# First MLP of a two-layer diffusion backbone: row sums moved from GpSimd to VectorE, background pieces placed by hand, two small rows loaded later

## Chip, cores and metric

The kernel runs on one core of a Trainium2 chip. The metric is the device time of one execution in microseconds (us); lower is better. The five engines of the core are called as in the profile: PE is TensorE, DVE is VectorE, ACT is ScalarE, POOL is GpSimd, SP is SyncE, which here only issues transfers. Each engine executes its own instructions strictly in their order; an instruction that waits holds up everything behind it on the same engine or issuing queue.

## What is computed

Two layers act on 512 latent tokens and 256 context tokens of width 1024. Layer 0 mixes tokens by pooling, layer 1 by attention; each is followed by an MLP with squared ReLU. The reference, cut to the part that the change touches (layer 0's MLP, on all 768 tokens):

```python
def ada_mods(cond, w, b):
    m = (jax.nn.silu(cond) @ w + b)[..., None, :]
    return jnp.split(m, N_MOD, axis=-1)
...
def sq_relu_mlp(h, w_in, w_out):
    return jnp.square(jax.nn.relu(h @ w_in)) @ w_out      # w_in 1024 x 4096, w_out 4096 x 1024
...
    m_lat = sq_relu_mlp(modulate(rms_norm(x, g_mlp_pre[i]), sh2, sc2), w_mlp_in[i], w_mlp_out[i])
    x = x + gt2 * rms_norm(m_lat, g_mlp_post[i])
```

The same MLP is applied to the context rows. `ada_mods` gives the shifts, scales and gates of each sub-layer; it needs silu(cond) for two conditioning vectors, `c` and `c_ctx`.

## The kernel before

**Precision.** Every float32 product is made of three products of halves: each operand is split into a rounded part (a CAST on ACT) and a remainder (a subtraction on DVE), and hi*hi + hi*lo + lo*hi is summed in PSUM.

**Front (0 to about 105 us).** Row norms, the pooling mixer and the conditioning of layer 0 run in an order written out by hand. SP streams the conditioning weights `w_ada` in 1 MB loads through a ring of six buffers (`raw_load`). `silu_rows` (L990) belongs to this kernel's later part but its four transfers carry no place of their own: for each of the two conditioning vectors, one writes silu(cond) as 1024 single floats to DRAM (`silu<-cond`, L992), and one reads that row back into all 128 partitions (`crow<-silu`, L993). The compiler's scheduler put the two writes at 12.54 us of the SP queue.

**First phase of the first MLP (about 105 to 387 us), `mlp0` (L1007).** The 4096 hidden columns are done in 16 rounds g of 256. Rounds 0 and 1 are plain. Rounds 2 to 15 use a seven-product scheme (Strassen's, in Winograd's form): instead of eight block products of half size, a round makes seven, each of 12 matmuls of 128x384 (`Seven`, L811; one such group is called a *half product* here, numbered 0 to 6). Half products 0, 2, 4 and 6 add into one PSUM bank `a`; between them ACT has to copy that bank out: `sc.copy(b, a)` after 0, `sc.copy(c, a)` after 2 (half product 4 may only start when that copy has read the bank), `sc.copy(r1[:, HN:TOK], a)` after 4 (half product 6 waits for it). At the end ACT applies ReLU and squares the two hidden rows into `hiddens[g % 2]`.

Between the half products, `behind(0)` to `behind(6)` issue background pieces:

- `weights_sums(g + 1, raw)` (L762) returns six steps that prepare the weights of the next round: `put` B11 (cast on ACT, remainder on DVE), `difference` (two DVE subtractions t1, t2 into a work tile), `put` T1 T2, `difference2` (t3, t4, into a second work tile; t4 reads the first one for the last time), `put3` T3 T4, `put3` B22.
- `asked` holds two calls of `ada_dot` (L340) per round: dot products of rows of `w_ada` with the rows `crow`, on DVE, two instructions (one per conditioning vector) for each call in rounds 2 to 13, one in rounds 14 and 15.

All pieces stand in one list, spread evenly: with eight pieces, `behind(0)` gets the first two, and the two dot calls come last, in `behind(5)` and `behind(6)`.

Work tiles rotate through three buffers (`work_tile`, L184). In one round they are first used in the order: t1/t2, `r1`, t3/t4, `r0`; so the ReLU into `r0` needs the buffer of t1/t2.

**Row sums.** Each pair of rounds (even, odd) gives the four quarters of a left operand of the second phase. `left_sums` (L975) runs after every odd round and before round 2 (seven times): POOL computes four sums of 128x768, and issues seven transfers per pair to DRAM (`lefts`), the three quarters and the four sums. Everything in this stretch is pinned to the written order on every engine (`pin(True)`).

**Loads.** A round asks SP for the weights of round g + 2 and then for the `w_ada` block of round g + 1. Both use a ring of three 1 MB buffers (`rawp`). Ahead of round 2 one of the three is held by the hidden rows of round 0 (`early`) until the first row sums have read them.

**Second phase, `Halves` (L1057, about 387 to 595 us).** The product with w_out again takes seven products per pair of rounds, in four passes, `PASSES = ((0, 4), (2, 5), (6, 3), (1,))`. A pass goes over the seven pairs with one or two of the products; each product keeps three PSUM banks for the whole pass, taken from two pools of four. `load` runs five products ahead, `prepare` three. At the last pair `take` (L1125) moves banks to SBUF; in product 5 it needs `self.banks[2]`, the banks of product 2.

Of the kernel before, what the change touches and what calls it, by code (L numbers as in the profile page):

```python
# [17 lines left out]
P = 128  # L18
# [79 lines left out]
def backbone(ctx: ExitStack, tc, x, ctx_in, w_ada, w_pool, w_qkv, g_q, g_k, w_o, w_mlp_in,  # L98
# [85 lines left out]
    def work_tile():  # L184
        return tmp.tile([P, D], F32, tag="t", name="work")
# [625 lines left out]
    class Seven:  # L811
# [10 lines left out]
        def run(self, behind):  # L822
            pool, tag = ((psB, "b"), (psA, "s"))[self.pool]
            b, a, c, e = (pool.tile([P, 512], F32, tag=tag, name="psin")[:, 0:HN] for _ in range(4))
            r0, r1 = (work_tile()[:, 0:TOK] for _ in range(2))
# [6 lines left out]
            self.chain(e, 1, True, True)  # L832
            sc.copy(r1[:, 0:HN], e)
# [4 lines left out]
            self.chain(b, 3, False, True)  # L838
            sc.activation(r0[:, 0:HN], b, AF.Relu)
# [49 lines left out]
    def keep(store, key, fn, *args):  # L889
        store[key] = fn(*args)  # L890
# [83 lines left out]

    def left_sums(p, even, odd):  # L975
        a11, a21, a12, a22 = (z[:, :, HN * h:HN * h + HN] for z in (even, odd) for h in range(2))
        s1, s2, s3, s4 = combined
        keep = lambda n, z: gp.dma_start(two(lefts[:, p, n]), z)
        def one(n, d, a, b, op):
            gp.tensor_tensor(out=d, in0=a, in1=b, op=op)  # L980
            keep(n, d)
        keep(0, a11)
        keep(1, a12)
        keep(3, a22)
        one(4, s1, a21, a22, ALU.add)
        one(5, s2, s1, a11, ALU.subtract)
        one(6, s3, a11, a21, ALU.subtract)
        one(2, s4, a12, s2, ALU.subtract)

    def silu_rows():  # L990
        for c in range(2):
            sy.dma_start(silu[c].rearrange("(k p) -> p k", p=P), cond[:, :, c])  # L992
            sy.dma_start(crow[:, c], silu[c].partition_broadcast(P))  # L993
# [7 lines left out]
    PASSES = ((0, 4), (2, 5), (6, 3), (1,))  # L1001
# [5 lines left out]
    def mlp0(inner, order, last, before_last):  # L1007
# [10 lines left out]
        inner = Inner(1, wi, hH, hL, hiddens[1], chunks0, TOK)  # L1018
        pinned[0] = False
        silu_rows()  # L1020
# [7 lines left out]
        left_sums(0, early, hiddens[1])  # L1028
        chain = Halves()
        for g in range(2, NG):  # L1030
            seven = Seven(products, hiddens[g % 2], g % 2, g < 4)
            pieces = []
            if g < NG - 1:
                steps, products = weights_sums(g + 1, raw)
                pieces += steps
            if asked:
                pieces += asked.pop(0)
            if g < NG - 2:
                raw = raw_load(w_mlp_in[0, g + 2])
            if g < NG - 1:  # L1040
                ask(*work.pop(0))
            else:
                chain.begin()
                pieces += [lambda: None] * 2 + [lambda: chain.prepare(0), lambda: None, lambda: chain.prepare(1)]
            n = len(pieces)
            seven.run(lambda z: [f() for f in pieces[(n * z + 6) // 7:(n * z + n + 6) // 7]])
            if g % 2 and g < 2 * PAIRS:
                left_sums(g // 2, *hiddens)
            if g == 4:
                head_gains()  # L1050
        chain.run()
# [5 lines left out]
    class Halves:  # L1057
# [67 lines left out]
        def take(self, n, q, ps):  # L1125
            c11, c12, c21, c22 = (accv[:, 2 * q + h, 512 * c:512 * c + 512] for h in range(2) for c in range(2))
            add = lambda d, a, b, op=ALU.add: ve.tensor_tensor(out=d, in0=a, in1=b, op=op)
            if n in (0, 4):
                sc.copy(c11 if n == 0 else c12, ps)
            elif n == 5:  # L1130
                add(c21, c11, ps)
                add(c22, c21, c12)
                add(c12, c22, self.banks[2][q])
            elif n == 6:
                add(c21, c21, ps)
                add(c22, c22, ps)
            elif n == 3:
                add(c21, c21, ps, ALU.subtract)
            elif n == 1:
                add(c11, c11, ps)  # L1140
# [202 lines left out]
    def head_gains():  # L1343
        tc.keep_in_program_order(sy.dma_start(grow[:, 0, :], g_q[0].partition_broadcast(P)))
        tc.keep_in_program_order(sy.dma_start(grow[:, 1, :], g_k[0].partition_broadcast(P)))
        ve.tensor_scalar(out=grow[:, 0, :], in0=grow[:, 0, :], scalar1=float(HD) ** -0.5, scalar2=None, op0=ALU.mult)
# [509 lines left out]
```

## Time and profile before

| quantity | value |
|---|---|
| median of 3 runs | 1198.72 us (1197.62 to 1199.57) |
| the profiled execution's own time | 1200.45 us |
| its span, first to last instruction | 1198.7 us, mean granted TensorE clock 0.974 |
| PE busy | 1124.0 us, 94% |
| DVE busy | 950.6 us, 79% |
| ACT busy | 618.0 us, 52% |
| POOL busy | 157.6 us, 13% |

How to read what the prediction quotes. A timeline row is: start in us from the span's start, duration in us, engine, line, operation, output<-input, partitions x elements, count, and in brackets the idle time just before it with what ended it. L94 is the line of a helper that records instructions in order, so rows are told apart by tile: `raw` is a loaded weight block, `work` a work tile, `units` and `rb` homes of prepared weights, `psin` the PSUM banks of the first phase, `pso` those of the second, `waste` the dots. A row of the waits view gives total wait, number of times and the longest. A row of the windows view gives a stretch, its length, then busy time (count) of PE, PEld (weight loads), DVE, ACT and POOL, the granted clock (1.00 is full), the share of the DMA engines and GB/s. A row of a DMA list ends with KB per transfer and the median time from issue to landing. A row of the groups gives total busy us and the mean ns of one.

### The profile page before, as it was taken

The page shows a single profiled execution, that of the slowest core. Times are in us where ns is not written, and L with a number is a line of the kernel's source. Part 1 is how long each engine was busy: PE and PEld are TensorE (multiplying, and loading weights), DVE is VectorE, ACT ScalarE, POOL GpSimd, SP SyncE. Part 2 cuts the span into 40 slices and gives each one's busy share as a digit, 9 for nine tenths or more (in the row PEclk, how much of TensorE's full clock was granted, in tenths as well). Part 3 has the DMA queues.
Part 4 walks back from the last instruction along what each step waited for, and adds up shares of the span by engine and source line. Part 5 has one row for each costly group of instructions (what it writes and reads, how often), then busy time and mean ns, then how long its engine had stood idle before and what let it go on. Part 6 is the DMA issues. An engine that isn't in the chain of part 4 may idle for free.

```text
span 1198.7 us, 15810 instructions
## 1 busy us (share of the span) xinstructions
PE 1124.0 (94%) x6030; PEld 979.7 (82%) x6030; DVE 950.6 (79%) x1291; ACT 618.0 (52%) x1035; POOL 157.6 (13%) x204
## 2 busy tenths in 40 slices
PE   7799789887898999899999999999999999999997
PEld 6479679877798787678888889998998888888886
DVE  5488888888886888898669678978687788779786
ACT  6387444434454553445358447764577345445523
POOL 1050332133321000000022220001200000000001
PEclk9899899888998999999999999999999999999999
DMA  9893555454557799997722210105334132313203
GB/s 365 281 388 118 185 198 188 156 210 180 202 176 270 303 366 393 383 361 271 279 110 71 71 36 19 61 28 193 123 125 157 36 141 108 110 64 141 106 19 122
DMA packets 52507, 213.13 MB, mean 178 GB/s; under 512 B 7408, under 2 KB 10304, under 8 KB 37840
## 3 DMA queue, kind: packets, MB, share of 16 engines
q1 hardware_dynamic: 45824, 185.52, 42.4%
q0 software_dynamic: 6608, 26.61, 5.7%
q8 instruction: 47, 0.77, 0.3%
q14 instruction: 28, 0.23, 0.1%
HBM read 178.16 MB, written 33.96 MB: 177 GB/s over the span
## 4 chain that ended last, share of the span: by engine, by line
PE 70%; DVE 15%; ACT 6%; issue 4%; DMA 3%; POOL 2%; SPq 0%; DVEq 0%; POOLq 0%; ACTq 0%
PE psin L682 14%; PE pso L94 12%; PE pso L1261 11%; PE psin L94 8%; DVE work L94 5%; PE pso L949 4%; PE psq L1385 4%; PE psy L1669 3%; PE po L1645 3%; DMA raw<-in_w_ada 3%; PE pss L1604 3%; DVE waste L94 3%; DVE units L94 3%; ACT units L94 2%; PE pspt L1626 2%
## 5 line engine op out<-in xcount | busy, mean ns | idle before, releaser
L94 PE MATMUL pso<-ra,sums 128*128 128x512 f32 x594 | 137.2, 390 | 3.8 <-DVE acc L94 3.5
L94 PEld LDWEIGHTS pso<-ra,sums 128*128 128x128 f32 x594 | 111.1, 188 | 28.8 <-DVE acc L94 4.3
L94 DVE CUSTOM_DVE_ANT_0 waste<-raw,crow 128x1024 f32<-128x1024 f32 (+1 forms) x72 | 88.1, 1224 | 8.5 <-DMA raw<-in_w_ada 6.8
L682 PE MATMUL psin<-ra,rb 128*128 128x512 f32 (+1 forms) x310 | 87.8, 360 | 0.0
L242 POOL TENSOR_SCALAR ms<-ss 128x1 f32<-128x1 f32 x15 | 9.7, 648 | 566.1 <-ACT junk L229 546.1
L1261 PE MATMUL pso<-units,pairs 128*128 128x512 f32 x336 | 82.7, 389 | 0.0
L682 PE MATMUL psin<-ra 128*128 128x512 f32 (+1 forms) x256 | 76.5, 376 | 0.0
L94 ACT CAST ra<-work 128x1024 fp32r<-128x1024 f32 x34 | 35.6, 1047 | 75.6 <-DVE work L94 73.9
L1261 PEld LDWEIGHTS pso<-units,pairs 128*128 128x128 f32 x336 | 63.1, 188 | 13.1
L1265 DVE TENSOR_TENSOR acc<-acc,pso 128x512 f32<-128x512 f32 x72 | 48.7, 682 | 26.2 <-PE pso L1261 26.2
L94 PE MATMUL psin<-sums,rb 128*128 128x384 f32 x70 | 27.8, 539 | 42.0 <-ACT psin L94 42.0
L94 PE MATMUL psin<-ra,units 128*128 128x384 f32 x340 | 63.5, 334 | 0.0
L682 PEld LDWEIGHTS psin<-ra,rb 128*128 128x128 f32 x310 | 55.6, 189 | 8.7
L94 PE MATMUL psin<-sums,units 128*128 128x384 f32 x336 | 61.2, 335 | 1.3 <-DVE units L772 0.6
L94 PEld LDWEIGHTS psin<-sums,units 128*128 128x128 f32 x336 | 58.3, 188 | 2.2 <-DVE units L772 1.0
L94 PE MATMUL pso<-ra,rb 128*128 128x512 f32 x252 | 58.6, 390 | 0.9 <-DVE ra L94 0.9
L94 PEld LDWEIGHTS psin<-ra,units 128*128 128x128 f32 x340 | 59.3, 188 | 0.0
L94 PEld LDWEIGHTS psin<-sums,rb 128*128 128x128 f32 x70 | 22.3, 327 | 44.2 <-ACT psin L94 44.2
L94 DVE TENSOR_TENSOR ra<-work,ra 128x1024 fp32r<-128x1024 f32 x34 | 41.7, 1225 | 19.3 <-ACT ra L94 19.3
L682 PE MATMUL psin<-rb,rb 128*128 128x512 f32 (+1 forms) x155 | 55.9, 362 | 0.6 <-DVE rb L1738 0.6
L94 PEld LDWEIGHTS pso<-ra,rb 128*128 128x128 f32 x252 | 47.2, 188 | 11.1 <-DVE ra L94 1.3
L94 ACT CAST units<-work 128x1024 fp32r<-128x1024 f32 x17 | 17.7, 1047 | 73.8 <-DVE work L94 67.8
(329 smaller groups left out, 2835.4 us busy)
## 6 DMA issues: line engine op xcount, KB each, us to landing
raw<-in_w_ada SPq DMA_DIRECT2D x48, 1024.0 KB, 10.3
raw<-in_w_mlp_in SPq DMA_DIRECT2D x32, 1024.0 KB, 5.1
lefts<-acc POOLq DMA_DIRECT2D x48, 384.0 KB, 3.3
raw<-in_w_mlp_out SPq DMA_DIRECT2D x18, 1024.0 KB, 5.5
wide<-lefts SPq DMA_DIRECT2D x38, 384.0 KB, 7.0
wide<-in_w_mlp_out SPq DMA_DIRECT2D x21, 512.0 KB, 7.0
halfway<-work POOLq DMA_DIRECT2D x14, 512.0 KB, 6.6
raw<-in_w_mlp_out SPq DMA_DIRECT2D x14, 512.0 KB, 7.3
```

Source lines behind the costliest of these rows:

```text
L94: return lambda *args, **kw: self.tc.keep_in_program_order(f(*args, **kw))
L242: gp.tensor_scalar(out=ms[:, 0:1], in0=ss[:, parts - 1:parts], scalar1=rest, scalar2=EPS, op0=ALU.add, op1=ALU.add)
L682: te.matmul(ps[:, bank, o:o + ln], w[:, k, fs], rhs, start=start, stop=(k == KT - 1 and n == 2), skip_group_check=len(ks) < KT or self.paired)
L949: te.matmul(pss[h][:, 0:cols[h][1]], a[:, f, ts_], w[:, f, cols[h][0]:sum(cols[h])], start=(n == 0 and not seeded[t]), stop=(n == len(seq) ...
L1261: te.matmul(ps, a, w, start=(m == 0), stop=(m == len(seq) - 1))
L1265: ve.tensor_tensor(out=M[n][:, t], in0=M[n][:, t], in1=ps, op=ALU.add)
L1385: te.matmul(ps, a[:, k, sl], w[:, k % 4, :], start=(k == 0 and n == 0), stop=(k == KT - 1 and n == 2))
L1604: te.matmul(ps[:, c2, 0:384], a[:, sl], b[:, kv, 384 * c2:384 * c2 + 384], start=(n == 0), stop=(n == 2))
L1626: te.transpose(ps[:, j, :], p[:, k * P:(k + 1) * P], ident)
L1645: te.matmul(po[:, 0:256], v, p, start=(n == 0), stop=(n == len(seq) - 1))
L1669: te.matmul(ps, a[:, k, sl], w[:, k % 4, o:o + width], start=(k == 0 and n == 0), stop=(k == KT - 1 and n == 2))
```

## The change

- `left_sums` no longer runs as a block on POOL. The four sums become four pieces for DVE, placed in the next even round behind half products 3, 4, 5 and 5. The transfers to `lefts` stay on POOL; the first quarter's is issued one round earlier (`left_keep`).
- The background pieces get fixed places: the six weight steps behind half products 0, 0, 1, 2, 3, 4; the two dot calls behind 1 and 6 (before: 5 and 6 in rounds with eight pieces). In the list behind half product 1 the dots stand after `put` T1 T2, ahead of `difference2`.
- `silu_rows` is called before the pin of the loads ends, and its four transfers are kept in the program's order on SP: behind the load of round 2's weights.
- `r1` and `r0` are taken from the rotation where they are first written.
- In the second phase the second pass handles product 5 before product 2; the addition into `c12` moves from product 5 to product 2.
- A scaling of `grow` moves from round 4 to round 8.

```diff
--- before.py
+++ after.py
@@ -822,7 +822,6 @@
         def run(self, behind):
             pool, tag = ((psB, "b"), (psA, "s"))[self.pool]
             b, a, c, e = (pool.tile([P, 512], F32, tag=tag, name="psin")[:, 0:HN] for _ in range(4))
-            r0, r1 = (work_tile()[:, 0:TOK] for _ in range(2))
             (wH, _), (aH, _) = self.products[0]
             for z in (b, c) if self.fresh else ():
                 te.matmul(z, wH[0], aH[0], start=True, stop=True, skip_group_check=True)
@@ -830,12 +829,14 @@
             sc.copy(b, a)
             behind(0)
             self.chain(e, 1, True, True)
+            r1 = work_tile()[:, 0:TOK]
             sc.copy(r1[:, 0:HN], e)
             behind(1)
             self.chain(a, 2, False, False)
             sc.copy(c, a)
             behind(2)
             self.chain(b, 3, False, True)
+            r0 = work_tile()[:, 0:TOK]
             sc.activation(r0[:, 0:HN], b, AF.Relu)
             behind(3)
             self.chain(a, 4, False, False)
@@ -972,25 +973,26 @@
     hiddens = [two(acc[:, 2 * TOK * q:2 * TOK * q + 2 * TOK]) for q in range(2)]
     combined = [two(acc[:, 4 * TOK + TOK * n:5 * TOK + TOK * n]) for n in range(4)]
 
+    def left_keep(p, n, z):
+        gp.dma_start(two(lefts[:, p, n]), z)
+
     def left_sums(p, even, odd):
         a11, a21, a12, a22 = (z[:, :, HN * h:HN * h + HN] for z in (even, odd) for h in range(2))
         s1, s2, s3, s4 = combined
-        keep = lambda n, z: gp.dma_start(two(lefts[:, p, n]), z)
+
         def one(n, d, a, b, op):
-            gp.tensor_tensor(out=d, in0=a, in1=b, op=op)
-            keep(n, d)
-        keep(0, a11)
-        keep(1, a12)
-        keep(3, a22)
-        one(4, s1, a21, a22, ALU.add)
-        one(5, s2, s1, a11, ALU.subtract)
-        one(6, s3, a11, a21, ALU.subtract)
-        one(2, s4, a12, s2, ALU.subtract)
+            ve.tensor_tensor(out=d, in0=a, in1=b, op=op)
+            left_keep(p, n, d)
+
+        left_keep(p, 1, a12)
+        left_keep(p, 3, a22)
+        return [lambda: one(4, s1, a21, a22, ALU.add), lambda: one(5, s2, s1, a11, ALU.subtract),
+                lambda: one(6, s3, a11, a21, ALU.subtract), lambda: one(2, s4, a12, s2, ALU.subtract)]
 
     def silu_rows():
         for c in range(2):
-            sy.dma_start(silu[c].rearrange("(k p) -> p k", p=P), cond[:, :, c])
-            sy.dma_start(crow[:, c], silu[c].partition_broadcast(P))
+            tc.keep_in_program_order(sy.dma_start(silu[c].rearrange("(k p) -> p k", p=P), cond[:, :, c]))
+            tc.keep_in_program_order(sy.dma_start(crow[:, c], silu[c].partition_broadcast(P)))
 
     asked = []
 
@@ -998,7 +1000,7 @@
         raw = raw_load(w_ada[i, m, j])
         asked.append([lambda b=b: ada_dot(i, m, j, nc_, raw, [crow[:, c] for c in range(nc_)], waste, b) for b in range(2)])
 
-    PASSES = ((0, 4), (2, 5), (6, 3), (1,))
+    PASSES = ((0, 4), (5, 2), (6, 3), (1,))
 
     def pin(on):
         for z in (ordered, mixed, queued):
@@ -1016,8 +1018,8 @@
         raw = raw_load(w_mlp_in[0, 2])
         steps, products = weights_sums(2, raw)
         inner = Inner(1, wi, hH, hL, hiddens[1], chunks0, TOK)
+        silu_rows()
         pinned[0] = False
-        silu_rows()
         for z in steps:
             z()
         inner.run()
@@ -1025,29 +1027,40 @@
         ask(*work.pop(0))
         sum_banks(True)
         pin(True)
-        left_sums(0, early, hiddens[1])
+        left_keep(0, 0, early[:, :, 0:HN])
+        due = left_sums(0, early, hiddens[1])
         chain = Halves()
         for g in range(2, NG):
             seven = Seven(products, hiddens[g % 2], g % 2, g < 4)
-            pieces = []
+            behind = [[] for _ in range(7)]
             if g < NG - 1:
                 steps, products = weights_sums(g + 1, raw)
-                pieces += steps
+                for n, z in enumerate(steps):
+                    behind[(0, 0, 1, 2, 3, 4)[n]].append(z)
+            if g % 2 == 0:
+                for n, z in enumerate(due):
+                    behind[(3, 4, 5, 5)[n]].append(z)
             if asked:
-                pieces += asked.pop(0)
+                for n, z in enumerate(asked.pop(0)):
+                    behind[(1, 6)[n]].append(z)
             if g < NG - 2:
                 raw = raw_load(w_mlp_in[0, g + 2])
             if g < NG - 1:
                 ask(*work.pop(0))
             else:
                 chain.begin()
-                pieces += [lambda: None] * 2 + [lambda: chain.prepare(0), lambda: None, lambda: chain.prepare(1)]
-            n = len(pieces)
-            seven.run(lambda z: [f() for f in pieces[(n * z + 6) // 7:(n * z + n + 6) // 7]])
-            if g % 2 and g < 2 * PAIRS:
-                left_sums(g // 2, *hiddens)
+                behind[4].append(lambda: chain.prepare(0))
+                behind[6].append(lambda: chain.prepare(1))
+            seven.run(lambda z: [f() for f in behind[z]])
+            if g < 2 * PAIRS:
+                if g % 2:
+                    due = left_sums(g // 2, *hiddens)
+                else:
+                    left_keep(g // 2, 0, hiddens[0][:, :, 0:HN])
             if g == 4:
                 head_gains()
+            if g == 8:
+                ve.tensor_scalar(out=grow[:, 0, :], in0=grow[:, 0, :], scalar1=float(HD) ** -0.5, scalar2=None, op0=ALU.mult)
         chain.run()
         pin(False)
         sum_banks(False)
@@ -1130,7 +1143,8 @@
             elif n == 5:
                 add(c21, c11, ps)
                 add(c22, c21, c12)
-                add(c12, c22, self.banks[2][q])
+            elif n == 2:
+                add(c12, c22, ps)
             elif n == 6:
                 add(c21, c21, ps)
                 add(c22, c22, ps)
@@ -1343,7 +1357,6 @@
     def head_gains():
         tc.keep_in_program_order(sy.dma_start(grow[:, 0, :], g_q[0].partition_broadcast(P)))
         tc.keep_in_program_order(sy.dma_start(grow[:, 1, :], g_k[0].partition_broadcast(P)))
-        ve.tensor_scalar(out=grow[:, 0, :], in0=grow[:, 0, :], scalar1=float(HD) ** -0.5, scalar2=None, op0=ALU.mult)
 
     kTH = kTL = vH = vL = early = None
```

## Prediction

> **What bounds the kernel now.** I read the page first (PE busy 94% of the span), then the waits of PE, then the windows of the first MLP, then the timeline of each engine over one even and one odd round.
>
> ```profile
> PE psin L94 <- ACT psin L94: 42.4, 8, 6.4
> 146.77:372.47 225.70, 190.17 (x1012) 187.37 (x1011) 189.93 (x227) 99.34 (x156) 70.96 (x66) 0.91 0.52 185
> ```
>
> PE's one large wait is that of the half products for a copy on ACT. Rounds 3 to 14, six pairs, take 225.7 us, 37.6 a pair, at a granted clock of 0.91. One even round on four engines, from its fourth half product:
>
> ```profile
> 280.76 2.25 PE L94 MATMUL psin<-ra,units 128*128 128x384 f32 x12
> 289.08 0.69 PE L94 MATMUL psin<-sums,rb 128*128 128x384 f32 x1 [6.08 <-ACT psin L94]
> 293.09 2.45 PE L94 MATMUL psin<-rb,rb 128*128 128x384 f32 x12
> 287.61 1.04 ACT L94 CAST units<-work 128x1024 fp32r<-128x1024 f32 x1 [8.20 <-DVE work L94]
> 282.45 2.29 DVE L94 TENSOR_TENSOR work<-raw 128x512 f32<-128x512 f32 x1
> 284.78 2.79 DVE L94 TENSOR_TENSOR work<-raw,work 128x512 f32<-128x512 f32 x1
> 282.16 2.04 POOL L94 TENSOR_TENSOR acc<-acc 128x768 f32<-128x768 f32 x1
> 285.20 1.81 POOL L94 TENSOR_TENSOR acc<-acc 128x768 f32<-128x768 f32 x1
> ```
>
> The chain reads backwards. PE waits 6.08 us for the copy into `c`; on ACT that copy stands behind a cast, which waited 8.20 us for DVE's t2; t1 and t2 took 2.29 and 2.79 us, ending just after POOL's sums end (284.20, 287.01). So POOL's row sums hold DVE up, and DVE holds PE. The odd round, which has no POOL sums:
>
> ```profile
> 301.73 1.23 DVE L94 TENSOR_TENSOR units<-raw,units 128x1024 fp32r<-128x1024 f32 x1 [0.43 <-ACT units L94]
> 303.59 0.69 DVE L94 TENSOR_TENSOR work<-raw,work 128x512 f32<-128x512 f32 x1
> 305.40 1.23 DVE L94 TENSOR_TENSOR units<-work,units 128x1024 fp32r<-128x1024 f32 x1 [1.12 <-ACT units L94]
> 307.15 0.69 DVE L94 TENSOR_TENSOR work<-raw,work 128x512 f32<-128x512 f32 x1
> 307.95 0.49 ACT L94 ACTIVATE work<-psin 128x384 f32<-128x384 f32 x1 [2.20 <-DVE work L94]
> 309.28 0.48 ACT L94 COPY work<-psin 128x384 f32<-128x384 f32 x1
> 309.41 1.23 DVE L94 TENSOR_TENSOR rb<-work,rb 128x1024 fp32r<-128x1024 f32 x1 [1.58 <-ACT rb L94]
> 308.01 2.24 PE L94 MATMUL psin<-rb,ra 128*128 128x384 f32 x12
> 310.09 2.24 PE L94 MATMUL psin<-ra 128*128 128x384 f32 x12
> 312.09 1.22 DVE L94 CUSTOM_DVE_ANT_0 waste<-raw,crow 128x1024 f32<-128x1024 f32 x1
> 314.96 0.48 ACT L94 COPY psin<-psin 128x384 f32<-128x384 f32 x1
> 315.37 1.05 ACT L94 CAST units<-raw 128x1024 fp32r<-128x1024 f32 x1
> 317.04 2.86 DVE L94 TENSOR_TENSOR units<-raw,units 128x1024 fp32r<-128x1024 f32 x1
> ```
>
> Without POOL beside it t2 takes 0.69 us. A half product takes 310.09 - 308.01 = 2.08 us; after the stop in the even round it was 293.09 - 289.08 = 4.01: the clock is lower there for a while. DVE goes from the first remainder (301.73) to that of the next round (317.04) in 15.3 us and ends without a gap before it; seven half products of 2.08 us are 14.6. DVE, not PE, already sets the pace of a round, with two waits for ACT in it (1.12 and 1.58). That decides what the change can give.
>
> **First MLP, even rounds.** Off: four POOL sums. On: four DVE sums of 768 elements.
>
> ```profile
> L94 DVE TENSOR_TENSOR sums<-wide,sums 128x768 fp32r<-128x768 f32 x28 | 26.7, 952 | 0.0
> 137.94 0.69 PE L94 MATMUL psin<-sums,rb 128*128 128x384 f32 x1 [6.45 <-ACT psin L94]
> 135.90 0.33 SPq L94 DMA_DIRECT2D raw<-in_w_mlp_in  x1
> DMA to landing us min/median/max: 4.7/5.0/6.8
> ```
>
> The nearest row gives 0.95 us each, four are 3.8 (at 1.23, the price of a 1024-wide one, 4.9). All else stays on DVE: 15.3 + 3.8 = 19.1 us for an even round. The sums stand behind half products 3 to 5, so the weight steps ahead of the critical copy run at their short times, and the 6.08 us stop goes. The seven transfers per pair stay on POOL; nothing waits behind them there, and the first quarter's is merely earlier.
>
> **First MLP, all rounds: the dots moved up.** Two dots (half of 312.09 to 317.04, 2.5 us) now lie on DVE ahead of t3 and t4. Who waits: the ReLU into `r0` takes the buffer of t1/t2, which t4 reads last (the 2.20 row). Behind that ReLU on ACT stand the cast of T3 T4 and the copy `r1` that half product 6 needs. From the first remainder to the ReLU is 307.95 - 301.73 = 6.2 us, now 8.7. From the ReLU to the end of that copy, 309.76, is 1.8; half product 6 starts then; from its start (310.09) through the last ReLUs, squares and the copy to the next round's first cast, ending 316.42, is 6.3; hand-overs 0.1. Sum 8.7 + 1.8 + 6.3 + 0.1 = 16.9 us. This loop exceeds DVE's own 15.3 and sets the odd rounds; in the even ones 19.1 is longer. The price of the move is thus 0 to 1.6 us per pair; I take 1.6, as every link has a row.
>
> A pair becomes 19.1 + 16.9 = 36.0 us against 37.6: 6 x 1.6 = 10 us saved. Round 2 loses its 6.45 us stop and 1.9 of slow products and gets a stop of 2.2 before half product 6 (2.5 of dots less the 0.3 in hand between 309.76 and 310.09): 6 saved. Against it: `early` is now read by the third sum, behind half product 5, and not by POOL at 136; the load that took its buffer at 135.90 goes out some 8 us later, lands 5 us after, and round 3's first cast waits about 3 (0 to 5). Sum for this phase: -10 - 6 + 3 = -13, between -28 (dots and load cost nothing, and the sums overlap a little) and -4 (the DVE sums cost 4.9 a pair, the load 5).
>
> The stops of PE that remain are thus some 2.2 us. [...]
>
> **Front: the silu rows.**
>
> ```profile
> 12.54 15.38 SPq L992 DMA_DIRECT2D silu<-cond  x2
> 28.02 12.77 SPq L179 DMA_DIRECT2D raw<-in_w_ada  x6
> DMA packets 2203, 0.88 MB, mean 68 GB/s; under 512 B 2097, under 2 KB 2097, under 8 KB 2097
> silu<-cond SPq DMA_DIRECT2D x2, 4.0 KB, 25.0
> 37.16 1.94 PE L94 MATMUL psada<-raw,cond 128*32 128x256 f32 x16 [5.58 <-DMA raw<-in_w_ada]
> 43.55 1.21 PE L94 MATMUL psada<-raw,cond 128*32 128x256 f32 x16 [2.65 <-DMA raw<-in_w_ada]
> 89.56 13.47 SPq L179 DMA_DIRECT2D raw<-in_w_mlp_in  x2
> 126.93 1.04 ACT L94 CAST units<-raw 128x1024 fp32r<-128x1024 f32 x1
> q1 hardware_dynamic: 1805, 8.87, 48.7%
> ```
>
> The two silu writes block the SP queue from 12.54 to 28.02, and in the DMA list of 28 to 41 us (the packet row) the core moves only 68 GB/s, with 2097 tiny packets. PE waits 5.58 + 2.65 = 8.2 us and then runs slow (sixteen products 1.94 us at first, 1.21 later: 0.7), which I count twice, 1.5, as the clock is still returning at 43.55. With the writes gone the loads follow one another. I take -10; bounds -12 (nearly all of the 13 us) and -5. In their new place the rows stand between the two loads of the 89.56 row, which then go at about 80 and 93; round 2's first cast of the second block (126.93) is then at 117. The two writes, at 13 us for both, and the wait of each read for its write fit into these 37 us, and the DMA list of 74 to 124 us (the last row) has its hardware queue busy only 48.7%: 0.
>
> **Second phase.**
>
> ```profile
> 509.98 1.66 PE L94 MATMUL pso<-ra,sums 128*128 128x512 f32 x6 [3.07 <-DVE acc L94]
> 512.03 5.75 PE L94 MATMUL pso<-ra,sums 128*128 128x512 f32 x24 [0.39 <-DVE acc L94]
> 448.61 0.69 SPq L94 DMA_DIRECT2D raw<-in_w_ada  x1
> 457.47 1.23 DVE L94 CUSTOM_DVE_ANT_0 waste<-raw,crow 128x1024 bf16<-128x1024 f32 x1 [1.16 <-DMA raw<-in_w_ada]
> ```
>
> After the second pass PE waits 3.07 + 0.39 = 3.5 us for the additions that free product 2's and 5's banks. With 5 first, its additions lie beside product 2, and product 2's beside product 6 of the next pass: -3.5. In exchange the buffer that a pair's load reuses is read last by product 2's remainder; from 5's subtraction to there lie two remainders of about 0.95 and one or two of 1.2, some 3 us. SP issues the `w_ada` load behind it, and the dots already wait 1.16 us for that (issued 448.61). Two buffers alternate, so at most 1.5 us per pair come through; I take half, over six pairs 4.5, and 0 if the three products prepared ahead hide it. Together +1, between -3.5 and +5.5. `grow`, moved to round 8, is one small instruction, free in both places.
>
> **Sum.** Against the profiled execution's 1200.45 us: -10 - 13 + 1 = -22, 1178.5. That execution lies 1.73 above the median shown, 1198.72; the forecast for the median is 1176.7. Own range: low 1200.45 - 12 - 28 - 3.5 - 1.7 = 1155; high 1200.45 - 5 - 4 + 5.5 - 1.7 = 1195.
>
> **Rivals.**
> - *Products set the pace.* If DVE's waits for ACT were filled, a pair would be fourteen half products, 29.1 us: 6 x 8.5 + 8 for round 2, less 3 for the load, is -56; with -10 and -3.5 the time is 1129. Against it: the odd rounds run without POOL and are at DVE's 15.3, not PE's 14.6. Chance 0.07.
> - *The first MLP gives nothing*: rounds about 1.1 us longer than worked out, as hand-overs on DVE and ACT add up. 1200.45 - 10 + 1 - 1.7 = 1190. For it: the forecast saves only 1.6 of 37.6 us a pair. Chance 0.12.
> - *The front's gain is lost*: the rows written in singles hold SP up again, now ahead of rounds 2 and 3's loads. The writes took 25 us to land at their old place; two of those behind each other and 5 for the load are 55 us where 37 are at hand, 18 too long: up to 1195. Against it: the half idle queue there. Chance 0.11.
> - *Slower: the clock falls at the short stops.* If 2.2 us idle are enough, half product 6 and the next 0 take 2.08 more each. In odd rounds both lie on the loop: after half product 6 (over at 312.33) ACT has only 2.6 us of its own, to 314.96, against the slower 4.2 of half product 0, so +2.1 and +1.6; in even rounds DVE's longer list leaves about +1.6. Per pair 5.3, with round 2 33 us in all: 1200.45 - 10 - 13 + 1 + 33 - 1.7 = 1210. It decides if stops of 2.2 us suffice. Against it: the stop of 3.07 us at 509.98 was followed by 24 products of 0.24 us, hardly slower than usual. Chance 0.07.
>
> The forecast's own chance is 0.60, and 0.03 is left for no change.
>
> **How the numbers follow.** The likeliest case gives 1176.7. The range 1155 to 1195 takes in its bounds and the two rivals on the near side; left out are the products' pace, the clock and the rest, 0.17. The measurement tells about 0.2% (2.4 us, so 1196.3) from no change. Faster: 0.60 + 0.07 + 0.12 + 0.09 of the third rival = 0.88; same: 0.03 + 0.02 = 0.05; slower 0.07.
>
> **What would show it.** Right: no POOL arithmetic between 125 and 375 us; t1 and t2 at 0.69 us in every round; PE's waits for ACT in the first MLP in many pieces near 2 us, before half product 6, in place of seven near 6; a pair near 36 us with even rounds longer than odd; the first `w_ada` waits gone and half the 28 to 41 us stretch's silence with them; no 3.07 us stop between the second and the third pass. Wrong: pairs near 29 or above 37 us, a granted clock in the first MLP that is still near 0.91, or SP rows of `silu` that end only after 110 us with round 2 waiting for its weights.

## The result, and the profile after

| | before | after |
|---|---|---|
| median | 1199.14 us (1197.62 to 1200.40, 4 runs) | 1181.98 us (1181.11 to 1186.17, 4 runs) |
| ratio | | 0.9864, 95% interval 0.9838 to 0.9891 |
| profiled execution, its span | 1200.45, 1198.7 us | 1181.55, 1179.4 us |
| mean granted clock | 0.974 | 0.992 |
| first matmul of the first MLP | 103.91 | 92.61 |
| from there to the first matmul of the second phase | 283.12 | 270.96 |
| from there to the first `psg` (L401) | 208.13 | 212.40 |
| from there to the end | 603.54 | 603.43 |

The change is faster by 1.4%; the whole interval lies below 1. The forecast for the median was 1176.7 us, in a range of 1155 to 1195. One of the four executions of a later run, dots_26, took 5709 us and the other three 1154.16 to 1155.64; that run's median below, 1155.51, counts the slow one (1155.38 without it), its ratio does not. The lower rows are differences of starts in PE's timeline and show where the time went: 11.3 us came from the front, 12.2 from the first phase of the first MLP, and 4.3 were given back in the second phase. Forecast were 10, 13 and a loss of 1.

The waits of PE over the whole span (total, times, longest), and a window of five pairs of rounds, from half product 6 of round 3 to that of round 13:

```profile
PE psin L94 <- ACT work L94: 23.3, 13, 2.0
PE psin L94 <- ACT psin L94: 10.4, 14, 2.6
147.54:329.27 181.73, 156.34 (x840) 149.60 (x841) 142.90 (x211) 83.45 (x131) 21.95 (x35) 0.97 0.53 193
```

The large stops near 6 us are gone. In their place stand thirteen of at most 2.0 us for ACT's copy `r1` (tile `work`), which is the stop before half product 6 that was forecast. A pair takes 181.73 / 5 = 36.35 us against 37.6, with the clock at 0.97 instead of 0.91. The timelines of PE, ACT and DVE show stops before half product 6, one whole even round (154.00 to 172.65) and both ends of an odd one (246.31 and 263.25):

```profile
164.49 2.35 PE L94 MATMUL psin<-ra,rb 128*128 128x384 f32 x12 [1.96 <-ACT work L94]
183.13 3.65 PE L94 MATMUL psin<-ra 128*128 128x384 f32 x12 [1.98 <-ACT work L94]
256.79 2.35 PE L94 MATMUL psin<-ra 128*128 128x384 f32 x12 [1.95 <-ACT work L94]
181.27 0.49 ACT L94 ACTIVATE work<-psin 128x384 f32<-128x384 f32 x1 [4.61 <-DVE work L94]
154.00 1.23 DVE L94 TENSOR_TENSOR units<-raw,units 128x1024 fp32r<-128x1024 f32 x1 [1.69 <-ACT units L94]
155.15 0.69 DVE L94 TENSOR_TENSOR work<-raw 128x512 f32<-128x512 f32 x1
158.82 1.22 DVE L94 CUSTOM_DVE_ANT_0 waste<-raw,crow 128x1024 f32<-128x1024 f32 x1
161.83 0.68 DVE L94 TENSOR_TENSOR work<-raw,work 128x512 f32<-128x512 f32 x1
164.09 1.22 DVE L94 TENSOR_TENSOR ra<-work,ra 128x1024 fp32r<-128x1024 f32 x1 [1.57 <-ACT ra L94]
165.23 0.95 DVE L94 TENSOR_TENSOR acc<-acc 128x768 f32<-128x768 f32 x1
172.65 1.22 DVE L94 TENSOR_TENSOR units<-raw,units 128x1024 fp32r<-128x1024 f32 x1
246.31 1.22 DVE L94 TENSOR_TENSOR units<-raw,units 128x1024 fp32r<-128x1024 f32 x1
263.25 1.22 DVE L94 TENSOR_TENSOR units<-raw,units 128x1024 fp32r<-128x1024 f32 x1 [1.27 <-ACT units L94]
```

t1 (155.15) is back at 0.69 us. A dot stands ahead of t4 (161.83), and ACT's ReLU into `r0` (181.27) waits 4.61 us in nearly every round; it starts 0.1 us after t4 ends each time. The sums (165.23) take 0.95 us. The even round that begins with the remainder at 154.00 ends at 172.65, after 18.65 us. The odd round from 246.31 to 263.25 takes 16.94; others take 18.0 to 18.25. Two products after the same stop show why: half product 6 took 2.35 us at 256.79, but 3.65 at 183.13, where the clock had dropped.

The front, in SP's timeline, the load that round 3 waits for, on ACT, and the second phase, on three engines:

```profile
6.09 25.59 SPq L179 DMA_DIRECT2D raw<-in_w_ada  x12
78.25 1.03 SPq L179 DMA_DIRECT2D raw<-in_w_mlp_in  x1
79.32 1.30 SPq L994 DMA_DIRECT2D silu<-cond  x1
91.38 0.34 SPq L179 DMA_DIRECT2D raw<-in_w_mlp_in  x1
92.64 0.42 SPq L994 DMA_DIRECT2D silu<-cond  x1
108.78 0.32 SPq L995 DMA_DIRECT2D crow<-silu  x1
135.98 1.05 ACT L94 CAST units<-raw 128x1024 fp32r<-128x1024 f32 x1 [1.99 <-DMA raw<-in_w_mlp_in]
427.73 0.42 SPq L94 DMA_DIRECT2D raw<-in_w_ada  x1
436.67 1.23 DVE L94 CUSTOM_DVE_ANT_0 waste<-raw,crow 128x1024 bf16<-128x1024 f32 x1 [2.74 <-DMA raw<-in_w_ada]
441.93 0.50 PE L94 MATMUL pso<-ra,sums 128*128 128x512 f32 x1 [1.72 <-ACT ra L94]
```

The first twelve `w_ada` loads go out without a break, and PE's waits of 5.58 and 2.65 us for them are gone. The first silu write now stands between the two weight loads and the second one behind both. Round 3's weights still go out at 91.38, before they are needed. In the second pass, DVE waits 2.74 us at once for the `w_ada` block issued at 427.73, and PE waits behind it.

### The profile page after: what moved, and what is told of

It reads as the page before. It is cut to its first block, busy times and chain, and to the rows that moved or that the text cites. A ratio compares the mean times of both kernels' runs of the same rounds, so it can differ in the third digit from the quotient of the medians.

```text
span 1179.4 us, 15819 instructions
## 1 busy us (share of the span) xinstructions
PE 1119.8 (95%) x6030; PEld 969.1 (82%) x6030; DVE 928.2 (79%) x1319; ACT 618.1 (52%) x1035; POOL 105.3 (9%) x176
## 4 chain that ended last, share of the span: by engine, by line
PE 72%; DVE 13%; ACT 6%; issue 4%; DMA 2%; POOL 2%; SPq 0%; ACTq 0%; DVEq 0%; POOLq 0%
PE psin L682 14%; PE pso L94 12%; PE pso L1275 11%; PE psin L94 9%; PE pso L950 5%; PE psq L1398 4%; PE psy L1682 3%; PE po L1658 3%; DVE work L94 3%; PE pss L1617 3%; DVE acc L94 2%; DVE waste L94 2%; PE pspt L1639 2%; DVE units L94 2%; DMA raw<-in_w_ada 1%
## 5 line engine op out<-in xcount | busy, mean ns | idle before, releaser
L94 ACT CAST ra<-work 128x1024 fp32r<-128x1024 f32 x34 | 35.6, 1047 | 83.3 <-DVE work L94 81.6
L94 PE MATMUL psin<-ra,units 128*128 128x384 f32 x340 | 65.8, 343 | 0.0
L94 PEld LDWEIGHTS psin<-ra,units 128*128 128x128 f32 x340 | 62.3, 196 | 0.0
L94 ACT ACTIVATE work<-psin 128x384 f32<-128x384 f32 x28 | 13.8, 492 | 91.5 <-PE psin L94 60.5
L94 DVE TENSOR_TENSOR ra<-work,ra 128x1024 fp32r<-128x1024 f32 x34 | 41.7, 1226 | 19.1 <-ACT ra L94 19.1
L682 PEld LDWEIGHTS psin<-ra 128*128 128x128 f32 x256 | 47.1, 188 | 8.7
L1398 PE MATMUL psq<-units,ra 128*128 128x512 f32 x216 | 52.4, 393 | 0.0
```

The lines of the kernel that those rows point to most:

```text
L94: return lambda *args, **kw: self.tc.keep_in_program_order(f(*args, **kw))
L682: te.matmul(ps[:, bank, o:o + ln], w[:, k, fs], rhs, start=start, stop=(k == KT - 1 and n == 2), skip_group_check=len(ks) < KT or self.paired)
L1398: te.matmul(ps, a[:, k, sl], w[:, k % 4, :], start=(k == 0 and n == 0), stop=(k == KT - 1 and n == 2))
```

## The experiments

Eleven kernels were run, in three groups; each group shares its runs of the kernel before (medians 1200.30, 1201.53 and 1203.43 us). The last three columns come from each profiled execution: the pair is the mean of four or five pairs.

| run | median us | ratio and 95% interval | pair us | first phase us | second phase us |
|---|---|---|---|---|---|
| the change | 1181.98 | 0.9864 [0.9838, 0.9891] | 36.35 | 270.96 | 212.40 |
| dots_late | 1172.00 | 0.9767 [0.9752, 0.9782] | 34.89 | 259.44 | 213.82 |
| sums_pool | 1213.22 | 1.0115 [1.0096, 1.0133] | 40.80 | 301.63 | 213.02 |
| passes_old | 1177.04 | 0.9807 [0.9791, 0.9823] | 36.42 | 271.55 | 207.52 |
| silu_old | 1193.65 | 0.9944 [0.9926, 0.9963] | 36.31 | 271.62 | 213.26 |
| combo | 1171.24 | 0.9749 [0.9726, 0.9772] | 35.49 | 262.09 | 211.10 |
| combo_mixed | 1167.33 | 0.9718 [0.9698, 0.9737] | 34.09 | 257.19 | 211.60 |
| dots_26 | 1155.51 | 0.9616 [0.9593, 0.9639] | 31.94 | 244.60 | 212.74 |
| sums_block | 1183.99 | 0.9854 [0.9829, 0.9879] | 36.78 | 272.39 | 212.46 |
| dots_36 | 1174.83 | 0.9772 [0.9754, 0.9789] | 35.27 | 263.15 | 212.31 |
| ends_first | 1153.07 | 0.9585 [0.9567, 0.9604] | 31.94 | 242.98 | 208.94 |
| gaps_filled | 1144.23 | 0.9515 [0.9494, 0.9536] | 30.87 | 236.56 | 210.28 |

**The silu rows at their old place (silu_old).**

```diff
-        silu_rows()
         pinned[0] = False
+        silu_rows()          # and its four transfers no longer kept in program order
```

> The changed kernel with one edit: the silu rows are issued after the pin of the loads ends, as before, so that the scheduler puts them ahead of the first w_ada loads. Theory (the two writes in single floats hold the SP queue in the front): the first MLP starts 11.3 us later, 1193. Rival (part of it is made good later, or the rows in their new place cost the first MLP something): 1184 to 1190. The first MLP starts at another time here, so that the places at which its clock falls may differ: six pairs without a fall are 213.6 us, each fall adds 1.3.

SP's timeline:

```profile
12.86 15.06 SPq L994 DMA_DIRECT2D silu<-cond  x2
```

The two writes hold the queue for 15 us again. The first MLP starts at 104.39 instead of 92.61, and the rest of the program is within 1.6 us of the change's. The front's gain stands alone and is not paid for later: 11.8 us by the starts, 11.7 by the medians.

**The dots behind 5 and 6 (dots_late).**

```diff
-                    behind[(1, 6)[n]].append(z)
+                    behind[(5, 6)[n]].append(z)
```

> The changed kernel with one edit: the two dot calls go back behind half products 5 and 6. Its own profile was 1181.55 us, its pairs 35.6 us, or 36.9 where the clock fell after a stop. Theory of the prediction (the dots ahead of t3 and t4 lengthen the loop t4, ReLU into r0, half product 6): the 2 us stops before half product 6 vanish, an odd round is DVE's own 15.3 us, an even one 15.3 + 3.8 = 19.1 or the 18.65 that was measured, a pair 34.0 to 34.4; with six pairs the profiled execution comes to about 1169. Rival A (DVE's total is all that counts, the place of the dots nothing): pair 35.6 to 36.9, 1181. Rival B (one stop of 4 us takes the place of several of 2 and brings the slow clock back in every even round): pair about 36, 1178, granted clock near 0.91 in the first MLP.

PE's and DVE's timelines of one odd round:

```profile
208.09 0.44 PE L94 MATMUL psin<-sums,ra 128*128 128x384 f32 x1 [3.26 <-ACT psin L94]
207.69 1.23 DVE L94 TENSOR_TENSOR units<-work,units 128x1024 fp32r<-128x1024 f32 x1 [1.11 <-ACT units L94]
211.69 1.23 DVE L94 TENSOR_TENSOR rb<-work,rb 128x1024 fp32r<-128x1024 f32 x1 [1.57 <-ACT rb L94]
```

The stops before half product 6 are gone, as the theory said, and the time falls by 10.0 us. So the dots' new place cost 10 us; it was no part of the gain. Rival B came in part: one stop of 3.3 us stands before half product 4 of each odd round, and four of the six from round 3 to round 13 were followed by slow products. The pair, 34.89 us, is above the forecast 34.0 to 34.4 mainly for that reason.

**The sums on POOL again (sums_pool).**

```diff
-            ve.tensor_tensor(out=d, in0=a, in1=b, op=op)
+            gp.tensor_tensor(out=d, in0=a, in1=b, op=op)
```

> The changed kernel with one edit: the four sums are computed on POOL again, at the same four places of the even round. Theory (an operation of POOL with two inputs and one of DVE hold each other up, so the sums cost the time of both): the weight steps t3, t4 and the remainders beside them take 1 to 2 us longer each, the even round becomes 15.3 plus up to 8 us, a pair 36.5 to 39, the time 1182 to 1198. Rival (only the place of the sums counted, and the engine that makes them does not): DVE is rid of 3.8 us in the even round, a pair is 33 to 34 us, the time about 1167.

POOL's and DVE's timelines at the head of an even round:

```profile
198.61 1.86 POOL L94 TENSOR_TENSOR acc<-acc 128x768 f32<-128x768 f32 x1
201.47 1.84 POOL L94 TENSOR_TENSOR acc<-acc 128x768 f32<-128x768 f32 x1
204.31 1.81 POOL L94 TENSOR_TENSOR acc<-acc 128x768 f32<-128x768 f32 x1
198.13 3.44 DVE L94 TENSOR_TENSOR units<-raw,units 128x1024 fp32r<-128x1024 f32 x1 [0.83 <-ACT units L94]
201.49 2.38 DVE L94 TENSOR_TENSOR work<-raw 128x512 f32<-128x512 f32 x1
203.90 2.78 DVE L94 TENSOR_TENSOR work<-raw,work 128x512 f32<-128x512 f32 x1
```

The time is 31 us above the change, and above the kernel before; 1182 to 1198 was expected. Each subtraction of DVE ends 0.6 to 1.1 us after the sum beside it: 1.23 us of work become 3.44, and 0.69 become 2.38 and 2.78. Each subtraction becomes 1.7 to 2.2 us longer, about one sum (1.81 to 1.86 us here). Whether DVE holds POOL up in turn was not shown: the four sums of the round all take 1.81 to 1.86 us. Which of the two starts first does not decide it in these rows: two of the three subtractions start 0.4 to 0.5 us before their sum and still end last. The expectation had t3 and t4 held up; it was t1 and t2, and with them the stop near 6 us before half product 4 came back. The places had no effect on POOL at all. The sums stand in the program behind half products 3, 4 and 5, but POOL, which had been idle for 16.25 us before the pair's first transfers, starts the first at 198.61, ahead of half product 3 (PE at 200.09), and all four before half product 4 (208.19), beside t1 and t2. On DVE, which is busy there, the place in the program did fix the time: in the change the first sum starts at 165.23, behind the remainder of T3 T4.

**The sums on DVE in one block (sums_block).**

```diff
-                for n, z in enumerate(due):
-                    behind[(3, 4, 5, 5)[n]].append(z)
+                for z in due:
+                    z()
```

> The changed kernel with the four sums on DVE in one block at the head of the even round instead of one by one behind half products 3, 4, 5 and 5. Theory of the prediction (the sums were placed behind half product 3 so that t1, t2 and the copy before half product 4 do not wait for them): a stop of 4 to 5 us before half product 4 of each even round, long enough to cost clock each time, a pair 36.5 to 38, the time 1182 to 1192. Rival (only DVE's sum counts): pair 35.6 to 36.9 as in the changed kernel, 1181.

PE's timeline, an even round before half product 4:

```profile
196.23 0.44 PE L94 MATMUL psin<-sums,rb 128*128 128x384 f32 x1 [2.30 <-ACT psin L94]
```

The time, 1183.99 us, and the pair, 36.78 us, lie in the ranges of the theory (the pair in the rival's as well), but the theory's mechanism came only in part: the stop before half product 4 grew to 1.1 to 2.3 us and not to 4 or 5, and the stops of 0.5 and 0.7 us before half products 2 and 4 of the odd round went. Placing the sums one by one brings about 2 us at most, and the two intervals overlap; the engine brings the rest.

**The first dots behind 2, and behind 3 (dots_26, dots_36).**

```diff
-                    behind[(1, 6)[n]].append(z)
+                    behind[(2, 6)[n]].append(z)      # dots_26; (3, 6) in dots_36
```

> The changed kernel with the first dot call behind half product 2 instead of 1, so behind t3 and t4 and ahead of the remainder of T3 T4. Theory (the dots cost because they delay t4, and with it the ReLU into r0): as good as late dots, no 2 us stops before half product 6, pair near 34.7, 1172. Rival (any dots ahead of a weight step cost the same): 1182, pair 35.6 to 36.9.

This expectation failed by 17 us, on the good side. DVE's timeline shows what both theories missed:

```profile
174.39 0.69 DVE L94 TENSOR_TENSOR work<-raw,work 128x512 f32<-128x512 f32 x1
174.99 1.22 DVE L94 CUSTOM_DVE_ANT_0 waste<-raw,crow 128x1024 f32<-128x1024 f32 x1
176.25 1.22 DVE L94 CUSTOM_DVE_ANT_0 waste<-raw,crow 128x1024 f32<-128x1024 f32 x1
177.41 1.22 DVE L94 TENSOR_TENSOR rb<-work,rb 128x1024 fp32r<-128x1024 f32 x1
```

Between t4 (174.39) and the remainder of T3 T4 (177.41), DVE used to wait 1.57 us for ACT's cast. Now two dots lie there, and the remainder follows without a wait. A theory was formed from this: the place is good because it covers a wait, not because it is early or late. The next run tested it.

> The changed kernel with the first dot call behind half product 3, so behind the remainder of T3 T4. With it behind 2 the time was 1155.5, a pair 31.9 us; behind 5, 1172.0 and 34.7. Theory (behind 2 the dots lie in the 1.57 us that DVE otherwise waits for the cast of T3 T4, twice a pair; nowhere else do they cover a wait): the two waits are back, a pair 34.5 to 35, the time 1170 to 1173. Rival (what counts is only that the dots come early enough to leave the end of the round free, and late enough not to delay t4): pair 32 to 32.5, the time 1155 to 1159.

The waits of DVE from 150 to 330 us, first for dots_36, then for dots_26:

```profile
DVE rb L94 <- ACT rb L94: 7.9, 5, 1.6
DVE ra L94 <- ACT ra L94: 7.9, 5, 1.6
```

```profile
DVE units L94 <- ACT units L94: 20.0, 17, 2.7
DVE ra L94 <- ACT ra L94: 0.4, 1, 0.4
```

One place later the two waits per pair are back (ten in this window), and with them 19 us. The time is 2 us above the expectation. Its stops of 2.8 us are followed by slow products in four of five pairs, but the one pair without them is as long (DVE's two rounds take 18.7 to 18.8 and 16.6 us in all of them), so that the clock does not explain the 19 us.

**The order of products 2 and 5 (passes_old, combo, combo_mixed, ends_first).** First, the old order alone:

> The changed kernel with one edit: the second pass handles product 2 before 5 again, with the addition to c12 in product 5. In the changed kernel the second phase takes 212.4 us against 208.1 before; the second pass is 65.7 us against 59.2, the other two 87.9 against 90.1. Theory (the new order makes the shared load wait longer, and the w_ada load and the dots behind it): the second phase is 208 us again, the stop of some 3 us after the second pass is back, the time is 1177. Rival (the order is worth its 2 to 3 us, and the second pass is long because the first MLP now ends earlier than the w_ada stream allows): second phase 213 to 216, time 1182 to 1185.

PE's timeline, the end of the second pass with the old order:

```profile
486.67 1.65 PE L94 MATMUL pso<-ra,sums 128*128 128x512 f32 x6 [3.11 <-DVE acc L94]
488.72 5.74 PE L94 MATMUL pso<-ra,sums 128*128 128x512 f32 x24 [0.39 <-DVE acc L94]
```

The stop of 3.1 us is back, and yet the second phase is 4.9 us shorter. The new order costs more in its loads than it saves at the boundary. Then the order was reversed in the last pair only, with the dots late (combo); in combo_mixed the dots of the even rounds stay behind 1. The edit, without the lines for the dots and for the loads' buffer:

```diff
-    PASSES = ((0, 4), (5, 2), (6, 3), (1,))
+    PASSES = ((0, 4), (2, 5), (6, 3), (1,))
-            self.todo = [(ps, p, n) for ps in range(len(PASSES)) for p in range(PAIRS) for n in PASSES[ps]]
+            self.todo = [(ps, p, n) for ps in range(len(PASSES)) for p in range(PAIRS)
+                         for n in (PASSES[ps][::-1] if ps == 1 and p == PAIRS - 1 else PASSES[ps])]
```

> The changed kernel with two edits: the dots behind half products 5 and 6, and in the second pass product 2 before 5 in the first six pairs but 5 before 2 in the last one, with the changed addition kept. Theory (each edit acts in its own stage, and only the last pair's order removes the stop between the passes): the first MLP as with late dots alone (1172.0), the second pass as in the old order, 59 us, and no 3.1 us stop at its end: 1172 - 5 - 3 = 1164. Rival A (only the old order acts, the stop stays): 1167. Rival B (a first MLP that ends earlier runs the second phase into its loads, as with late dots alone, where PE waited 3.93 us once): 1168 to 1171.

> As the run with both edits, but the dots stand behind half products 1 and 6 in even rounds, as in the changed kernel, and behind 5 and 6 in odd rounds. DVE's list is as long, but its shortage of 4 us a pair should come as stops of 2 us and less instead of one of 3.3. [...] Rival (only DVE's sum counts): the same as that run. Rival (the loop through t4 costs in even rounds as well): 3 to 8 us above it.

PE's timeline at the same place, in combo:

```profile
478.94 9.39 PE L94 MATMUL pso<-ra,sums 128*128 128x512 f32 x30 [4.08 <-DVE acc L94]
```

The expected 8 us did not come (1171.24 against 1172.00), and rival B's reason is not the cause either. In the second phase the loads were better, but product 6 shares its pool of banks with the product that is named first in the pass before. That was now product 2, which ended last, so the stop grew to 4.08 us, and the 30 products after it were slow (9.39 us, 0.31 each, against 8.32 for the next 36, 0.23 each). The second phase took 211.10 us, 2.7 under dots_late. The first phase, the same program as in dots_late, took 2.7 longer, with six stops followed by slow products against four. In combo_mixed the second phase has the same fault, with a stop of 2.45 us. Its first phase is 4.9 us shorter than combo's, with the same sum of work on DVE: a pair is 34.09 against 35.49 us, with one such stop against six. Expected were 34.4 to 34.7 us and at most 2 us less time than combo; it was 3.9. So part of what the placement of the dots decides is the clock. With the banks of the change kept, and the dots behind 2 (one line of the edit):

```diff
+                         for n in (PASSES[ps][::-1] if ps == 1 and 0 < p < PAIRS - 1 else PASSES[ps])]
```

> The first dot call behind half product 2, and in the second pass product 5 before 2 only in the first and the last pair, 2 before 5 in the five between; product 2 keeps the banks that it has in the changed kernel, so that the next pass does not wait for the banks of the product that ended last. With the dots alone the time was 1155.5 and the second phase 212.7 us; with the old order it was 207.5 and had a stop of 3.1 us at the end of the pass. Theory (five of the seven pairs load late because of the order, and the end of the pass is set by the last pair alone): second phase 204 to 208, the time 1147 to 1151. Rival (as in the run with two edits, the stop moves or grows): 210 to 213, 1153 to 1156.

The second phase is 208.94 us, 3.8 under dots_26 and without a stop above 0.8 us at the boundary. By the ratios the whole gain is about 0.3%, and the two intervals overlap. Second phase and time (1153.07 us) are both slower than expected; the time lies in the rival's range, though no stop between the passes moved or grew.

**The other wait filled (gaps_filled).** The edit against the run before it, without the lines that take the dot calls apart:

```diff
-                    behind[(3, 4, 5, 5)[n]].append(z)
+                    behind[(0, 4, 5, 5)[n]].append(z)
-                    behind[(2, 6)[n]].append(z)
+                    behind[((0 if g % 2 else 2, 2, 6, 6) if len(q) == 4 else (2, 6))[n]].append(z)
```

> As the run before it, and the 1.11 us that DVE waits in every round for the cast of T1 T2 is filled as well: with the first sum in even rounds (behind half product 0 instead of 3), with one dot product of the first call in odd rounds (the calls are taken apart into single dot products). Theory (DVE sets the pace through its list and its waits for casts): the even round loses 0.95, the odd one 1.1 us, a pair 29.9 against 31.9 us, just above the 29.1 of fourteen half products; 12 us under the run before it. Rival (another wait, the stops of PE before half products 2 and 4, sets the pace now): 0 to 4 us under it.

Windows of four pairs, in dots_26 and then in gaps_filled:

```profile
173.04:300.79 127.75, 119.95 (x673) 116.11 (x673) 113.88 (x171) 67.00 (x104) 17.57 (x28) 1.00 0.64 225
```

```profile
170.40:293.88 123.48, 119.47 (x672) 116.20 (x672) 113.75 (x171) 66.74 (x104) 17.57 (x28) 1.00 0.64 230
242.85 1.23 DVE L94 TENSOR_TENSOR units<-raw,units 128x1024 fp32r<-128x1024 f32 x1 [1.45 <-ACT units L94]
```

A pair is 30.87 against 31.94 us, a gain of half the size that was expected; the time fell by 8.8 us and not by 12. The even round lost 0.9 us, as it should; the odd one went from 14.9 to 14.7, and DVE waits 1.45 us at its end (the row at 242.85). There the seven half products of 2.08 us, 14.6 us, set the pace. This is the fastest version, 1144.23 us, 4.9% under the kernel before and 3.5% under the change by the ratios.

## Why the prediction was right, and where it was wrong

**Front, -10.** Measured -11.3, shown by the run with the old place. The loads went out in one stretch, and the rows in single floats did not delay the loads behind them in their new place: neither ACT nor DVE waits for a load between 76 and 130 us there. The two writes took 12.9 and 16.1 us to land, where the third rival reckoned with 25 each.

**Round 2 and its load, -6 + 3.** From the start of round 2 (120.56 and 109.25) to half product 6 of round 3 (159.59 and 147.54) the gain is only 0.7 us. The stop of round 2 went as worked out and left stops of 0.56 and 1.98 us. But round 3 waited for its load, as forecast: ACT's cast 1.99 us and PE 2.62. It waited a further 1.95 before its own half product 6: the loop's price was counted only from the pairs after it.

**Pairs, 36.0 us.** The even round was given 19.1 and took 18.65; the odd one 16.9, and took 16.94 where the clock held. Such a pair takes 35.6 us. In three of the five pairs of the window the clock fell at the stop before half product 6, and these take 36.8 to 36.9: each fall costs 1.3 us. Over the five pairs the gain is 6.3 us against 8; from half product 6 of round 13 to the second phase it is 5.2 (39.46 to 34.30), not 1.6, which fits that the last two rounds have half the dots: round 14 stops only 0.31 us before half product 6. That the phase as a whole, 12.2 us, comes so near the 13 of the forecast is thus in part luck: round 2 and the five pairs gave 4 us less than worked out, and the end 3.6 more. The loop through t4 is shown by dots_late, dots_26 and dots_36, none of which has a 2 us stop before half product 6. Whether the buffer of `r0` or the cast of T3 T4 holds the copy was not separated: both wait for t4.

**The clock.** The prediction gave stops of 2.2 us a chance of 0.07 to cost clock, as "2.2 us idle" would have to be enough every time. Against it stood one stop of 3.07 us that cost nothing, and one case was too few. The rival was true in part: of the thirteen stops before half product 6 in the change, four were followed by slow products. The rival's 2.08 us more for each of two half products is shown by no run: after the stop at 183.13 the first took 3.65 us against 2.35, the second 2.57 against 2.24. In the thirteen profiles, PE stopped 230 times in the first phase for more than 0.3 us between 118 and 350 us; a stop is called slow if the next 24 products took over 0.22 us each, without the waits between them, against 0.18:

| stop, us | stops | followed by slow products |
|---|---|---|
| under 1.7 | 136 | 0 |
| 1.7 to 2.05 | 54 | 17 |
| 2.05 to 3.0 | 16 | 7 |
| 3.0 to 3.5 | 12 | 10 |
| over 5.8 | 12 | 12 |

So no stop under 1.7 us cost clock (0 of 136), each one over 5.8 did (12 of 12), and between the two the length alone does not decide: of two stops of 1.98 us in the change, the one at 127.17 was followed by products of 0.18 us and the one at 183.13 by products of 0.24. What decides there was not shown; no run set the place of a stop on purpose. combo_mixed came off well: of its six stops of 1.95 to 1.98 us between 126 and 299 us, one was followed by slow products, where all runs together have 17 of 54 in that row.

**Second phase, +1.** Measured +4.3. Both terms were there with the right sign, and both sizes were off. In PE's timeline, where each of the first passes has 252 matmuls, the second grew from 59.5 to 65.8 us, 6.3 against 4.5, so that of the 1.5 us per pair seven tenths came through and not half; the passes after it gained 2.0 against 3.5, because waits of 0.50 and 0.77 us stand there in place of the 3.46.

**"DVE, not PE, already sets the pace of a round."** This is the step that misjudged what was possible. It put DVE's 15.3 us down as its own, "with two waits for ACT in it", and then kept these waits whatever was moved. The price of the change came out right, as its dots lie where they cover no wait. But the rival in which "DVE's waits for ACT were filled" got 0.07 for the change and no thought as an edit: one place further on, two dots fill the 1.57 us and a pair falls to 31.9 us; with the 1.11 us filled too, to 30.9, where the products (29.1) are near.

## What to carry to other kernels

A wait of the engine that sets the pace is a place, not a fixed cost: before moving side work, look for the rows in which that engine waits for another one, and put pieces of about that length there. Here program order fixed the time of the sums on DVE, which was busy, and not on POOL, which was idle and started the first at 198.61, ahead of the half product 3 (200.09) that it stands behind. Side work should not go to an engine that holds up the one that sets the pace, as POOL's sums did here (t1 and t2 took 2.38 and 2.78 us beside them, 0.69 alone). In this kernel, stops of PE under 1.7 us each cost no clock (0 of 136); longer ones are worth splitting, since those of 1.7 to 2.05 us were followed by slow products in 17 of 54 cases and those of 3.0 to 3.5 in 10 of 12. combo_mixed, which did so, had one of six.

## What the runs showed that was not expected

- Of PE's stops of 1.7 to 2.05 us, 17 of 54 were followed by slow products, in the change at about 1.3 us each, and a stop of 3.45 us cost no clock in dots_late (before half product 4 of round 3). What tells them apart was not shown.
- The sums on POOL met t1 and t2 although they stood in the program behind half products 3 to 5, and cost more than the whole change gains (1213.22 us against 1200.30 before).
- Which PSUM pool a product's banks come from decided a 4.08 us stop between two passes, in a run whose order of work had been made to avoid a 3.1 us one.
